# Experts' stage of a two-block model: rows written back half a block later, slot lists four experts at a time, inner columns stored in the order of their transposes

## Chip, cores and metric

The kernel runs on 1 core of one Trainium2 chip. The metric is the device time of one execution in microseconds (us), the median of several; less is better.

## What is computed

Two transformer blocks on 256 tokens of width 1024 in 32-bit floats. The first block's second layer has a mixture of experts, and the change lies there: each token goes to 2 of 8 experts, each expert is a gated network of inner width 3584, and the results are weighted and added to the tokens. Cut to that part:

```python
def moe_swiglu(h, w_router, w_gate, w_up, w_down):
    ...
    logits = (xt @ w_router).astype(jnp.float32)
    top_logit, top_idx = lax.top_k(logits, TOP_K)
    gates = jax.nn.softmax(top_logit, axis=-1)
    ...
    xs = xt_pad[tok_buf].reshape(n_blocks, EXPERT_BLOCK, D)

    def expert_block(args):
        xb, e = args
        return swiglu(xb, w_gate[e], w_up[e], w_down[e])

    ys = lax.map(expert_block, (xs, block_expert)).reshape(rows, D)
    ys = ys * gate_buf[:, None].astype(ys.dtype)
    out = jnp.zeros((T + 1, D), ys.dtype).at[tok_buf].add(ys)[:T]
    return out.reshape(B, S, D)

def swiglu(h, w_gate, w_up, w_down):
    return (jax.nn.silu(h @ w_gate) * (h @ w_up)) @ w_down
```

Before the experts come attention, a dense network and a convolution; after them a second block with two kinds of attention and a dense network.

## The kernel before

**Precision and weights.** Each large product is made of three matmuls (`mm3`, lines 408 to 410): high half times high half, low times high, high times low. All weights come through one stream (`Stream`). SP issues transfers of 1 MB into a ring of raw buffers (tile `wraw`, line 93; 13 buffers in the experts' stage). ScalarE makes the high half of a unit (`whi`, line 107), VectorE subtracts it from the raw weights for the low half (`wlo`, line 122). There are five pairs of `whi` and `wlo`; the stream prepares up to four units ahead of TensorE. In the experts' stage a unit is one slice of 128 rows by 1024 columns, which feeds six matmuls.

**An expert.** Its inner width is cut into blocks 0 to 3 (three of 1024 columns, one of 512). For each block TensorE does, in this order: the gate column into PSUM banks 0 and 1 (`expert_col(gb, ...)`), the up column into banks 2 and 3, then the down product of the block before (`gemm_row` with `prev`), which adds into banks 4 and 5. ScalarE applies the activation to the gate (line 1634), VectorE multiplies it with up (line 1640); both write the tile `grow`. `turn_pairs` then transposes the block's inner values through banks 2 and 3 (line 1621) and splits them into `hth` and `htl` (`split`, lines 389 and 390) for the next block's down product. The down weights are stored in pairs of rows, so the inner columns are turned in even and odd halves: the transposes read `grow` with a stride of two words.

**Handing over.** In block 0 of the next expert the last down product of the one before ends. `rows_of` then copies its rows from banks 4 and 5 into `xn` as high and low halves; `places` makes the slot pattern `ptok` from the slot list; `combine(..., n)` writes one half (n) of the columns back to the tokens: four matmuls of `xn` with `ptok` (line 1537) and two VectorE updates of `h` (line 1540). Half 0 stands at the end of block 0, half 1 behind the gate column of block 1.

**Slot lists.** `slots` finds for each expert which token lies in which slot. It compares (tile `oneb`, line 1490), multiplies with the token numbers (line 1495) and writes `slotv` and `slotr`. `fetch` gathers the next expert's rows by `slotr` on POOL (line 1502), and `turned` transposes them in block 3. All eight experts' lists are made at the end of expert 0's block 1, with the gate weights (`gates`) and the counts (`counts`).

The order on each engine is the order of the code: the schedule is written by hand, and only semaphores delay an instruction.

Of the kernel before, what the change touches and what calls it, by code (L numbers as in the profile page):

```python
# [10 lines left out]
F32 = mybir.dt.float32  # L11
F32R = mybir.dt.float32r
BF = mybir.dt.bfloat16
I32 = mybir.dt.int32
U32 = mybir.dt.uint32
AF = mybir.ActivationFunctionType
OP = mybir.AluOpType
# [4 lines left out]
D = 1024  # L22
# [7 lines left out]
NE = 8  # L30
# [133 lines left out]
def two_blocks(tc, A, out):  # L164
# [14 lines left out]
    def bank(i, shape=(128, 512)):  # L179
        return psp.tile(list(shape), F32, name=f"b{i}", tag=f"b{i}", bufs=1)  # L180
# [126 lines left out]
    R = {}  # L307
# [80 lines left out]
    def split(src, hi_, lo_):  # L388
        S.activation(hi_, src, AF.Copy)  # L389
        V.tensor_tensor(lo_, src, hi_.bitcast(F32), op=OP.subtract)  # L390

    def turn(*a):
        run(turns(*a))
# [48 lines left out]
    def gemm_row(o, ht, chunks, first, last, outer=False, tbs=(0, 1), lead=0):  # L442

        th, tl = ht
        nch = len(chunks)

        def one(u, i, tb, n):
            wh, wl = u
            c = chunks[i]
            mm3(o[tb][n], th[:, c, tb * 128:tb * 128 + 128], tl[:, c, tb * 128:tb * 128 + 128],  # L450
                wh[:, 0, n * 512:n * 512 + 512], wl[:, 0, n * 512:n * 512 + 512],
                first and i == 0, last and i == nch - 1)

        if outer:


            us = []
            for tb in tbs:
                seq = [(n, i) for i in range(nch if tb != tbs[-1] else lead) for n in range(2)]
                seq += [(n, i) for n in range(2) for i in range(len(seq) // 2, nch)]  # L460
                for j, (n, i) in enumerate(seq):
                    if tb == tbs[0] and i >= len(us):
                        us += W.take(1 if lead else nch)
                    one(us[i], i, tb, n)
                    if tb == tbs[-1] and n == 1:
                        W.done(1)
                    if j % 2:
                        yield
        else:
            for i in range(nch):  # L470
                u = W.take(1)[0]
                for tb in tbs:
                    for n in range(2):
                        one(u, i, tb, n)
                    if tb == tbs[-1]:
                        W.done(1)
                    yield

    def run(g):
        for _ in g:  # L480
            pass
# [958 lines left out]
    def gates():  # L1440
        V.tensor_tensor(gg[:, :, 0], mxv[:, :, 1], mxv[:, :, 0], op=OP.subtract)
        S.activation(gg[:, :, 0], gg[:, :, 0], AF.Exp)
        V.tensor_scalar(gg[:, :, 1], gg[:, :, 0], 1.0, None, op0=OP.add)
        V.reciprocal(gg[:, :, 1], gg[:, :, 1])
        V.tensor_tensor(gg[:, :, 2], gg[:, :, 0], gg[:, :, 1], op=OP.mult)
        for tb in range(2):
            V.tensor_scalar(gate[:, tb], oh[:, tb, 0], gg[:, tb, 1:2], None, op0=OP.mult)
            V.scalar_tensor_tensor(gate[:, tb], oh[:, tb, 1], gg[:, tb, 2:3], gate[:, tb], op0=OP.mult, op1=OP.add)
# [31 lines left out]
                  xe[1][:, g * 4:g * 4 + 4])  # L1480
        return xe

    def slots():

        b = bank(7)
        for e0 in range(0, NE, 4):
            ps = []
            for tb in range(2):
                p = mp.tile([128, 4, 128], BF, name="oneb")
                V.tensor_tensor(p, iota[:, None, 1:129].to_broadcast([128, 4, 128]),  # L1490
                                place[:, tb, e0:e0 + 4, None].to_broadcast([128, 4, 128]), op=OP.is_equal)
                ps.append(p)
            for x in range(4):
                for tb in range(2):
                    PE.matmul(b[:, e0 + x:e0 + x + 1], ps[tb][:, x], tokv[:, tb:tb + 1], start=tb == 0, stop=tb == 1)
        V.tensor_copy(slotv, b[:, 0:NE])
        V.tensor_scalar(slotr, slotv, -1.0, 0.0, op0=OP.add, op1=OP.max)

    def fetch(e):

# [4 lines left out]
    def turned(x):  # L1505
        xe = new_xe()
        turn(x, 8, xe[0], xe[1], 0, 0, [6, 7])
        return xe

    def places(e):  # L1510

        pt = mp.tile([128, T], F32R, name="ptok", bufs=1)
        V.tensor_scalar(pt, iota[:, 1:257], slotv[:, e:e + 1], None, op0=OP.is_equal)
        return pt
# [9 lines left out]
    def rows_of(acc):  # L1524

        y = [scr.tile([128, D], F32R, name="xn") for i in range(2)]
        for n in range(2):
            c = slice(n * 512, n * 512 + 512)
            split(acc[n], y[0][:, c], y[1][:, c])
        return y  # L1530

    def combine(e, y, pt, n, tbs=(0, 1)):

        for tb in tbs:
            b = bank(6 + (tb + n) % 2)
            for i, v in enumerate(y):
                PE.matmul(b, pt[:, tb * 128:tb * 128 + 128], v[:, n * 512:n * 512 + 512], start=i == 0,
                          stop=i == len(y) - 1)
            hv = h[:, tb, n * 512:n * 512 + 512]
            V.scalar_tensor_tensor(hv, b, gate[:, tb, e:e + 1], hv, op0=OP.mult, op1=OP.add)  # L1540

    def counts():
        cnt = m1.tile([128, 8], F32, name="cnt")
        b = bank(6)
        for tb in range(2):
            PE.matmul(b[:, 0:8], onesb, sel[:, tb], start=tb == 0, stop=tb == 1)
        mxc = m1.tile([128, 1], F32, name="mxc")
        V.tensor_copy(cnt, b[:, 0:8])
        V.reduce_max(mxc, cnt, axis=AX.X)
        mci = m1.tile([128, 1], I32, name="mci")  # L1550
        V.tensor_copy(mci, mxc)
        return mci
# [54 lines left out]
    def expert_col(bks, xe, n):  # L1607

        if n == 512:
            run(gemm_col([bks[0]], xe, n, tbs=(0,)))  # L1610
        else:
            run(gemm_row([bks], xe, list(range(8)), True, True, tbs=(0,)))

    def turn_pairs(sg, n, ht):


        v = sg[:, 0:n].rearrange("t (q p c) -> t q c p", p=128, c=2)
        for q in range(0, n // 256, 2):
            b = bank(2 + q // 2)
            for x in range(4):  # L1620
                PE.transpose(b[:, x * 128:x * 128 + 128], v[:, q + x // 2, x % 2], ident)
            split(b.rearrange("p (j t) -> p j t", t=128), ht[0][:, 2 * q:2 * q + 4], ht[1][:, 2 * q:2 * q + 4])

    prev = last = None
    nfi = len(exp_blocks)
    for e in range(NE):
        xe = xes.pop(e)
        for fi, (c0, n) in enumerate(exp_blocks):
            hs = [slice(x, x + 512) for x in range(0, n, 512)]
            gb, ub = [bank(0), bank(1)], [bank(2), bank(3)]  # L1630
            expert_col(gb, xe, n)
            sg = growp.tile([128, D], F32, name="grow")
            for x, c in enumerate(hs):
                S.activation(sg[:, c], gb[x], AF.Silu)
            if last is not None:
                combine(*last, 1)
                last = None
            expert_col(ub, xe, n)
            for x, c in enumerate(hs):
                V.tensor_tensor(sg[:, c], ub[x], sg[:, c], op=OP.mult)  # L1640
            if fi == nfi - 1 and e + 1 < NE:
                xes[e + 1] = turned(xg)
            if prev is not None:
                pe_, pacc, pht, pfi, pn = prev
                run(gemm_row([pacc], pht, list(range(pn // 128)), pfi == 0, pfi == nfi - 1, tbs=(0,)))
                if pfi == nfi - 1:
                    last = (pe_, rows_of(pacc), places(pe_))
            if e == 0 and fi == 1:
                gates()
                mci = counts()  # L1650
                slots()
                gcol = const.tile([128, 16], F32, name="gcol")
                for i, nm in enumerate(("mixg", "ffng")):
                    V.scalar_tensor_tensor(gcol[:, 8 * i:8 * i + 8], colsA[:, 8 + 24 * i:16 + 24 * i], 1.0,
                                           P[:, R[nm]:R[nm] + 8], op0=OP.add, op1=OP.mult)
            if fi == min(e, 1) ^ 1 and e + 1 < NE:
                xg = fetch(e + 1)
            if fi == 0:
                acc = [bank(4), bank(5)]
            ht = tuple(mp.tile([128, 8, 128], F32R, name=f"ht{x}", bufs=1) for x in "hl")  # L1660
            turn_pairs(sg, n, ht)
            prev = (e, acc, ht, fi, n)
            if last is not None:
                combine(*last, 0)
    pt = places(NE - 1).bitcast(F32)
    overflow()
    W.hold = True
    for j, _ in enumerate(gemm_row([acc], prev[2], list(range(prev[4] // 128)), False, True, outer=True, tbs=(0,),
# [428 lines left out]
```

## Time and profile before

| | before |
|---|---|
| median of 3 runs | 1856.91 us (1853.91 to 1859.42) |
| profiled execution | 1855.81 us, span 1854.0 us |
| granted TensorE clock, mean | 0.987 |
| TensorE matmuls busy | 1792.2 us, 97% of the span |
| VectorE busy | 1472.1 us, 79% |
| ScalarE busy | 1230.0 us, 66% |
| read from memory | 504.93 MB, 273 GB/s over the span |

The span is the profiled execution from its first to its last instruction; the rest of its time lies around it. Shares of the span are means over stages with different limits: the experts' stage runs from about 515 to 1500 us, and there VectorE and the memory traffic are busier than the table says. A TensorE that is shown as busy has pipelined matmuls whose ends are modelled, so the distance from start to start tells more than the duration.

### The profile page before, as it was taken

What the parts mean: (1) busy time and instruction counts of PE and PEld (TensorE: products, weight loads), DVE (VectorE), ACT (ScalarE), POOL (GpSimd) and SP (SyncE); (2) the same over time, 40 slices, a digit from 0 to 9 for tenths busy, and PEclk for the clock granted to TensorE, in tenths of its full rate; (3) what the DMA queues carried; (4) which work ended last, traced back from release to release, by engine and by line L of the source; (5) the groups of instructions that cost most, each with busy time, mean ns of one, the idle gap of its engine ahead of it and who ended that gap; (6) DMA issues with size and microseconds to landing.
All of it is one profiled execution on the core that took longest, in us unless ns stands there. A gap on an engine that the chain in (4) does not pass through costs nothing. (4 is left out here: it accounts for less than half of the span.)

```text
span 1854.0 us, 23616 instructions
## 1 busy us (share of the span) xinstructions
PE 1792.2 (97%) x8614; PEld 1488.0 (80%) x8614; DVE 1472.1 (79%) x1759; ACT 1230.0 (66%) x1597; POOL 47.4 (3%) x72
## 2 busy tenths in 40 slices
PE   7999999999998999999999999999999989999998
PEld 6788888889787878888788788887887867778886
DVE  5556988688788999999999999999999974477553
ACT  5644444476477778878788778787887866556442
POOL 1100000000100000000000000000000010010000
PEclk9999999999999999999999999999999999999999
DMA  7324998562598999999999999999999735237540
GB/s 276 137 80 158 396 352 296 182 217 80 206 345 315 382 353 360 383 345 367 369 360 379 358 364 377 344 361 363 357 367 357 274 110 172 91 102 264 191 160 23
DMA packets 162740, 508.65 MB, mean 274 GB/s; under 512 B 8452, under 2 KB 26040, under 8 KB 148280
## 3 DMA queue, kind: packets, MB, share of 16 engines
q1 hardware_dynamic: 160200, 499.37, 73.8%
q0 software_dynamic: 2128, 7.18, 1.2%
q8 instruction: 69, 1.13, 0.2%
q10 hardware_dynamic: 288, 0.52, 0.1%
q14 instruction: 55, 0.45, 0.1%
HBM read 504.93 MB, written 2.11 MB: 273 GB/s over the span
## 5 line engine op out<-in xcount | busy, mean ns | idle before, releaser
L122 DVE TENSOR_TENSOR wlo<-wraw,whi 128x1024 fp32r<-128x1024 f32 (+1 forms) x894 | 1063.8, 1220 | 178.7 <-ACT whi L107 132.3
L107 ACT ACTIVATE whi<-wraw 128x1024 fp32r<-128x1024 f32 (+1 forms) x894 | 935.0, 1059 | 304.9 <-PE b L409 280.7
L408 PE MATMUL b<-whi,xeh 128*128 128x512 f32 x896 | 352.2, 393 | 0.0
L410 PE MATMUL b<-wlo,xeh 128*128 128x512 f32 x896 | 350.3, 391 | 0.0
L409 PE MATMUL b<-whi,xel 128*128 128x512 f32 x896 | 350.2, 391 | 0.0
L408 PE MATMUL b<-whi,hth 128*128 128x512 f32 x664 | 262.6, 395 | 0.9 <-ACT hth L389 0.9
L408 PE MATMUL b<-whi,xth 128*128 128x512 f32 (+2 forms) x656 | 257.1, 392 | 6.3 <-ACT xth L389 2.3
L409 PE MATMUL b<-whi,htl 128*128 128x512 f32 x664 | 261.4, 394 | 0.4 <-DVE htl L390 0.4
L410 PE MATMUL b<-wlo,hth 128*128 128x512 f32 x664 | 261.5, 394 | 0.0
L409 PE MATMUL b<-whi,xtl 128*128 128x512 f32 (+2 forms) x656 | 251.6, 384 | 1.7 <-DVE xtl L390 0.9
L410 PE MATMUL b<-wlo,xth 128*128 128x512 f32 (+2 forms) x656 | 251.2, 383 | 1.1 <-DVE wlo L122 1.1
L410 PEld LDWEIGHTS b<-wlo,xeh 128*128 128x128 f32 x896 | 168.7, 188 | 35.2
L408 PEld LDWEIGHTS b<-whi,xeh 128*128 128x128 f32 x896 | 169.2, 189 | 34.6
L409 PEld LDWEIGHTS b<-whi,xel 128*128 128x128 f32 x896 | 168.9, 189 | 34.6
L408 PEld LDWEIGHTS b<-whi,xth 128*128 128x128 f32 x656 | 125.8, 192 | 32.1 <-ACT xth L389 3.8
L408 PEld LDWEIGHTS b<-whi,hth 128*128 128x128 f32 x664 | 126.3, 190 | 27.4 <-ACT hth L389 1.4
L409 PEld LDWEIGHTS b<-whi,htl 128*128 128x128 f32 x664 | 126.1, 190 | 27.0 <-DVE htl L390 1.1
L410 PEld LDWEIGHTS b<-wlo,hth 128*128 128x128 f32 x664 | 126.2, 190 | 26.7
L410 PEld LDWEIGHTS b<-wlo,xth 128*128 128x128 f32 x656 | 125.6, 191 | 25.6 <-DVE wlo L122 2.5
L409 PEld LDWEIGHTS b<-whi,xtl 128*128 128x128 f32 x656 | 125.6, 191 | 24.6 <-DVE xtl L390 2.7
L389 ACT ACTIVATE hth<-b 128x512 fp32r<-128x512 f32 (+1 forms) x84 | 45.9, 591 | 70.8 <-PE b L401 38.6
L390 DVE TENSOR_TENSOR htl<-b,hth 128x512 fp32r<-128x512 f32 (+1 forms) x84 | 54.1, 681 | 39.8 <-ACT hth L389 39.8
(357 smaller groups left out, 1399.9 us busy)
## 6 DMA issues: line engine op xcount, KB each, us to landing
wraw<-in_moe_w_gate_dram SPq DMA_DIRECT2D x112, 1024.0 KB
wraw<-in_moe_w_up_dram SPq DMA_DIRECT2D x112, 1024.0 KB
wraw<-in_moe_w_down_dram SPq DMA_DIRECT2D x112, 1024.0 KB
wraw<-in_w_ff_dram SPq DMA_DIRECT2D x32, 1024.0 KB
adw<-in_ada_w_dram SPq DMA_DIRECT2D x24, 1024.0 KB
wraw<-in_w_in_dram SPq DMA_DIRECT2D x12, 1024.0 KB
wraw<-in_ffn_w_gate_dram SPq DMA_DIRECT2D x11, 1024.0 KB
wraw<-in_ffn_w_up_dram SPq DMA_DIRECT2D x11, 1024.0 KB
```

Source lines behind the costliest of these rows:

```text
L107: nc.scalar.activation(h, r, AF.Copy)
L122: self.nc.vector.tensor_tensor(l, r, h.bitcast(F32), op=OP.subtract)
L389: S.activation(hi_, src, AF.Copy)
L390: V.tensor_tensor(lo_, src, hi_.bitcast(F32), op=OP.subtract)
L408: PE.matmul(o, xh, wh, start=first, stop=False)
L409: PE.matmul(o, xl, wh, start=False, stop=False)
L410: PE.matmul(o, xh, wl, start=False, stop=last)
```

## The change

The half-0 write-back moves from the end of block 0 to behind the gate column of block 1, and half 1 from there to behind the up column. The `ptok` pattern is made in block 2 of the expert itself. The slot lists are made in two goes of four experts (expert 0 and expert 1), the compare in block 0, the matmuls in block 1. The activation and the product write `grow` in the order in which it is turned, so they read PSUM with a stride of two words and the transposes read contiguous columns. The first block's transposes move behind the next gate column, into banks 6 and 7. The gather of the next rows is issued in block 2. The core of the diff:

```diff
-    def slots():
+    def slots(e0):
+        ps = []
+        for tb in range(2):
+            p = mp.tile([128, 4, 128], BF, name="oneb")
+            V.tensor_tensor(p, iota[:, None, 1:129].to_broadcast([128, 4, 128]),
+                            place[:, tb, e0:e0 + 4, None].to_broadcast([128, 4, 128]), op=OP.is_equal)
+            ps.append(p)
+        yield
         b = bank(7)
...
+        for x in range(4):
             for tb in range(2):
+                PE.matmul(b[:, x:x + 1], ps[tb][:, x], tokv[:, tb:tb + 1], start=tb == 0, stop=tb == 1)
+        V.tensor_copy(slotv[:, e0:e0 + 4], b[:, 0:4])
+        V.tensor_scalar(slotr[:, e0:e0 + 4], slotv[:, e0:e0 + 4], -1.0, 0.0, op0=OP.add, op1=OP.max)
+        yield
...
-    def turn_pairs(sg, n, ht):
-        v = sg[:, 0:n].rearrange("t (q p c) -> t q c p", p=128, c=2)
-        for q in range(0, n // 256, 2):
-            b = bank(2 + q // 2)
-            for x in range(4):
-                PE.transpose(b[:, x * 128:x * 128 + 128], v[:, q + x // 2, x % 2], ident)
-            split(b.rearrange("p (j t) -> p j t", t=128), ht[0][:, 2 * q:2 * q + 4], ht[1][:, 2 * q:2 * q + 4])
+    def pairs(x):
+        return x.rearrange("t (q p c) -> t q c p", p=128, c=2)
+    def turn_pairs(sg, n, ht, bk):
+        turn(sg, n // 128, ht[0], ht[1], 0, 0, bk)
...
+        sv4 = [sg[:, x:x + 512].rearrange("t (q c p) -> t q c p", p=128, c=2) for x in hs]
+        for x, v in enumerate(sv4):
+            S.activation(v, pairs(gb[x]), AF.Silu)
+        if later is not None:
+            later()
+            later = None
+        if last is not None:
+            combine(*last, 0)
+        expert_col(ub, xe, n)
+        for x, v in enumerate(sv4):
+            V.tensor_tensor(v, pairs(ub[x]), v, op=OP.mult)
+        if last is not None:
+            combine(*last, 1)
+            last = None
...
-                    last = (pe_, rows_of(pacc), places(pe_))
+                last = (pe_, rows_of(pacc), pt)
...
+        if e < 2 and fi in (0, 1):
+            next(sl[e])
+        if fi == 2:
+            if e + 1 < NE:
+                xg = fetch(e + 1)
+            pt = places(e)
...
-            if last is not None:
-                combine(*last, 0)
```

On VectorE, at the end of block 0 of expert 1 and into block 1, the kernel before has this order (`xn` are the low halves of expert 0's rows, `htl` those of the transposes, `h` the tokens, `wlo` the low halves of weights):

```order
L122 TENSOR_TENSOR wlo<-wraw,whi 128x1024 x4
L390 TENSOR_TENSOR xn<-b_4835,xn 128x512
L390 TENSOR_TENSOR xn<-b_4836,xn 128x512
L1513 TENSOR_SCALAR ptok<-iota,slotv 128x256
L390 TENSOR_TENSOR htl<-b_5932,hth 128x512
L390 TENSOR_TENSOR htl<-b_5939,hth 128x512
L1540 SCALAR_TENSOR_TENSOR h<-b_5946,gate,h 128x512
L1540 SCALAR_TENSOR_TENSOR h<-b_5950,gate,h 128x512
```

And the changed kernel at the same place:

```order
L122 TENSOR_TENSOR wlo<-wraw,whi 128x1024 x4
L390 TENSOR_TENSOR xn<-b_4839,xn 128x512
L390 TENSOR_TENSOR xn<-b_4840,xn 128x512
L1488 TENSOR_TENSOR oneb<-iota,place 128x512 x2
L390 TENSOR_TENSOR htl<-b_5922,hth 128x512
L390 TENSOR_TENSOR htl<-b_5929,hth 128x512
L122 TENSOR_TENSOR wlo<-wraw,whi 128x1024 x8
L1541 SCALAR_TENSOR_TENSOR h<-b_6031,gate,h 128x512
L1541 SCALAR_TENSOR_TENSOR h<-b_6035,gate,h 128x512
L122 TENSOR_TENSOR wlo<-wraw,whi 128x1024 x8
L1647 TENSOR_TENSOR grow<-b_5938,grow 128x512
L1647 TENSOR_TENSOR grow<-b_5939,grow 128x512
```

The pattern `ptok` has left this place, the first two updates of `h` stand eight conversions later, and in expert 1 alone two compare patterns have come in. The other two updates follow the last product shown.

On TensorE, at the same boundary, the kernel before:

```order
L410 MATMUL b_4836<-wlo,hth 128x512
L1621 MATMUL b_5932<-ident,grow 128x128 x4
L1621 MATMUL b_5939<-ident,grow 128x128 x4
L1537 MATMUL b_5946<-xn,ptok 128x512 x2
L1537 MATMUL b_5950<-xn,ptok 128x512 x2
L408 MATMUL b_5954<-whi,xeh 128x512
```

The changed kernel there:

```order
L410 MATMUL b_4840<-wlo,hth 128x512
L401 MATMUL b_5922<-ident,grow 128x128 x4
L401 MATMUL b_5929<-ident,grow 128x128 x4
L408 MATMUL b_5936<-whi,xeh 128x512
L409 MATMUL b_5936<-whi,xel 128x512
```

and a gate column later:

```order
L409 MATMUL b_5937<-whi,xel 128x512
L410 MATMUL b_5937<-wlo,xeh 128x512
L1538 MATMUL b_6031<-xn,ptok 128x512 x2
L1538 MATMUL b_6035<-xn,ptok 128x512 x2
L408 MATMUL b_5938<-whi,xeh 128x512
```

The four row matmuls have moved from between the transposes and the gate column to between the gate and the up column.

On VectorE, at the end of expert 0's block 1, the kernel before makes the patterns and the lists in one go (`cnt` and `mci` belong to the counts):

```order
L1548 COPY cnt<-b_5136 128x8
L1549 TENSOR_REDUCE mxc<-cnt 128x1
L1551 CAST mci<-mxc 128x1
L1490 TENSOR_TENSOR oneb<-iota,place 128x512 x4
L1496 COPY slotv<-b_5144 128x8
L1497 TENSOR_SCALAR slotr<-slotv 128x8
```

The changed kernel has there:

```order
L1549 COPY cnt<-b_5140 128x8
L1550 TENSOR_REDUCE mxc<-cnt 128x1
L1552 CAST mci<-mxc 128x1
L1663 SCALAR_TENSOR_TENSOR gcol<-colsA,P 128x8 x2
L1496 COPY slotv<-b_5151 128x4
L1497 TENSOR_SCALAR slotr<-slotv 128x4
```

The compare patterns stand before this place now: two of them behind the product of block 0, the other two in expert 1, as shown above.

## Rows read from the trace of the kernel before

**Rows 1.** Timeline, POOL: one gather; start, duration, idle time before and releaser.

```profile
1118.81 0.94 POOL L1502 DMA_INDIRECT zN<-zD,slotr  x1 [121.54 <-PE b L401]
```

**Rows 2.** Windows, one expert: length, PE, PEld, DVE, ACT, POOL busy, clock, DMA share, GB/s.

```profile
1000.00:1122.48 122.48, 120.76 (x549) 100.45 (x549) 113.39 (x109) 97.22 (x102) 0.94 (x1) 1.00 0.98 366
```

**Rows 3.** Waits from 600 to 1450: who waited for whom, us, times, longest.

```profile
SPq L93 <- DVE wlo L122: 722.0, 292, 5.8
ACT whi L107 <- PE b L409: 142.1, 424, 2.5
...
PE b L1537 <- ACT whi L107: 12.0, 7, 1.7
```

**Rows 4.** Timeline: two gate transfers are issued, and the gate column that uses them starts.

```profile
666.08 2.64 SPq L93 DMA_DIRECT2D wraw<-in_moe_w_gate_dram  x2
...
705.38 0.48 PE L408 MATMUL b<-whi,xeh 128*128 128x512 f32 x1
```

**Rows 5.** Timeline, PE and DVE: the end of expert 1's block 0.

```profile
667.10 1.11 PE L1621 MATMUL b<-ident,grow 128*128 128x128 f32 x8
...
668.24 1.29 DVE L390 TENSOR_TENSOR xn<-b,xn 128x512 fp32r<-128x512 f32 x2
...
669.43 0.35 DVE L1513 TENSOR_SCALAR ptok<-iota,slotv 128x256 fp32r<-128x256 f32 x1
...
669.93 1.17 PE L1537 MATMUL b<-xn,ptok 128*128 128x512 f32 x4 [1.72 <-ACT whi L107]
...
670.94 0.39 PE L408 MATMUL b<-whi,xeh 128*128 128x512 f32 x1
...
672.32 0.39 PE L408 MATMUL b<-whi,xeh 128*128 128x512 f32 x1
```

**Rows 6.** Timeline, PE: the second half of the same rows, behind the gate column.

```profile
681.84 1.07 PE L1537 MATMUL b<-xn,ptok 128*128 128x512 f32 x4
...
682.75 0.39 PE L408 MATMUL b<-whi,xeh 128*128 128x512 f32 x1
```

**Rows 7.** Timeline, PE: eight transposes at stride two, the next matmul, eight contiguous ones.

```profile
615.66 1.11 PE L1621 MATMUL b<-ident,grow 128*128 128x128 f32 x8
616.53 0.48 PE L408 MATMUL b<-whi,xeh 128*128 128x512 f32 x1
...
627.55 1.03 PE L401 MATMUL b<-ident,zN 128*128 128x128 f32 x8
```

**Rows 8.** Groups from 600 to 1450: count, busy us, mean ns, idle before.

```profile
L122 DVE TENSOR_TENSOR wlo<-wraw,whi 128x1024 fp32r<-128x1024 f32 x585 | 695.5, 1223 | 53.9 <-ACT whi L107 18.7
...
L1640 DVE TENSOR_TENSOR grow<-b,grow 128x512 f32<-128x512 f32 x49 | 31.7, 683 | 0.0
L1621 PEld LDWEIGHTS b<-ident,grow 128*128 128x128 f32 x196 | 27.8, 205 | 2.2
...
L1540 DVE SCALAR_TENSOR_TENSOR h<-b,gate,h 128x512 f32<-128x512 f32 x28 | 19.7, 745 | 0.0
...
L401 PEld LDWEIGHTS b<-ident,zN 128*128 128x128 f32 x56 | 6.5, 140 | 0.9
```

**Rows 9.** Timeline, PE: counts, slot lists and the next gate column, expert 0.

```profile
572.91 0.20 PE L1546 MATMUL b<-sel,onesb 128*128 128x8 bf16 x2
...
576.67 0.18 PE L1495 MATMUL b<-tokv,oneb 128*128 128x1 bf16 x1 [3.56 <-DVE oneb L1490]
...
577.27 0.33 PE L1495 MATMUL b<-tokv,oneb 128*128 128x1 bf16 x7 [0.42 <-DVE oneb L1490]
...
580.78 0.77 PE L408 MATMUL b<-whi,xeh 128*128 128x512 f32 x1
```

**Rows 10.** Windows behind that place, columns as in rows 2.

```profile
580.00:582.00 2.00, 2.00 (x9) 1.80 (x8) 0.90 (x2) 1.43 (x3) 1.14 (x2) 0.50 0.19 73
...
584.00:586.00 2.00, 2.00 (x8) 1.56 (x7) 1.22 (x1) 0.71 (x2) 0.00 (x0) 0.69 0.74 266
```

**Rows 11.** Timeline, PE: expert 0's first transposes.

```profile
539.02 1.34 PE L1621 MATMUL b<-ident,grow 128*128 128x128 f32 x8 [1.43 <-DVE grow L1640]
```

More of the change, by code (lines that the diff above doesn't have):

```diff
@@ L1481, in gather @@
         return xe
-    def slots():
+    def slots(e0):
[6 more added lines that the diff above has]
+        yield
         b = bank(7)
-        for e0 in range(0, NE, 4):
-            ps = []
+        for x in range(4):
             for tb in range(2):
[L1489 to L1492, printed above, removed]
-            for x in range(4):
[L1494 to L1497, printed above, removed]
+                PE.matmul(b[:, x:x + 1], ps[tb][:, x], tokv[:, tb:tb + 1], start=tb == 0, stop=tb == 1)
+        V.tensor_copy(slotv[:, e0:e0 + 4], b[:, 0:4])
+        V.tensor_scalar(slotr[:, e0:e0 + 4], slotv[:, e0:e0 + 4], -1.0, 0.0, op0=OP.add, op1=OP.max)
+        yield
     def fetch(e):
@@ L1612, in expert_col @@
             run(gemm_row([bks], xe, list(range(8)), True, True, tbs=(0,)))
-    def turn_pairs(sg, n, ht):
-        v = sg[:, 0:n].rearrange("t (q p c) -> t q c p", p=128, c=2)
-        for q in range(0, n // 256, 2):
-            b = bank(2 + q // 2)
-            for x in range(4):
-                PE.transpose(b[:, x * 128:x * 128 + 128], v[:, q + x // 2, x % 2], ident)
-            split(b.rearrange("p (j t) -> p j t", t=128), ht[0][:, 2 * q:2 * q + 4], ht[1][:, 2 * q:2 * q + 4])
+    def pairs(x):
+        return x.rearrange("t (q p c) -> t q c p", p=128, c=2)
@@ L1624, in two_blocks @@
+    def turn_pairs(sg, n, ht, bk):
+        turn(sg, n // 128, ht[0], ht[1], 0, 0, bk)
     prev = last = None
     nfi = len(exp_blocks)
[L1626 to L1634, printed above, removed]
-            if last is not None:
[L1636 to L1646, printed above, removed]
-                    last = (pe_, rows_of(pacc), places(pe_))
[L1648 to L1656, printed above, removed]
-                xg = fetch(e + 1)
[L1658 to L1663, printed above, removed]
-                combine(*last, 0)
@@ L1665, in two_blocks, with later @@
-    pt = places(NE - 1).bitcast(F32)
+    steps = [(e, fi) for e in range(NE) for fi in range(nfi)]
+    later = None
+    sl = [slots(0), slots(4)]
+    for e, fi in steps:
+        c0, n = exp_blocks[fi]
+        if fi == 0:
+            xe = xes.pop(e)
+        hs = range(0, n, 512)
+        gb, ub = [bank(0), bank(1)], [bank(2), bank(3)]
+        expert_col(gb, xe, n)
+        sg = growp.tile([128, D], F32, name="grow")
+        sv4 = [sg[:, x:x + 512].rearrange("t (q c p) -> t q c p", p=128, c=2) for x in hs]
[3 more added lines that the diff above has]
+            later()
+            later = None
+        if last is not None:
[6 more added lines that the diff above has]
+            last = None
+        if fi == nfi - 1 and e + 1 < NE:
+            xes[e + 1] = turned(xg)
+        if prev is not None:
+            pe_, pacc, pht, pfi, pn = prev
+            run(gemm_row([pacc], pht, list(range(pn // 128)), pfi == 0, pfi == nfi - 1, tbs=(0,)))
+            if pfi == nfi - 1:
+                last = (pe_, rows_of(pacc), pt)
+        if e == 0 and fi == 1:
+            gates()
+            mci = counts()
+            gcol = const.tile([128, 16], F32, name="gcol")
+            for i, nm in enumerate(("mixg", "ffng")):
+                V.scalar_tensor_tensor(gcol[:, 8 * i:8 * i + 8], colsA[:, 8 + 24 * i:16 + 24 * i], 1.0,
+                                       P[:, R[nm]:R[nm] + 8], op0=OP.add, op1=OP.mult)
+        if e < 2 and fi in (0, 1):
+            next(sl[e])
+        if fi == 2:
+            if e + 1 < NE:
+                xg = fetch(e + 1)
+            pt = places(e)
+        if fi == 0:
+            acc = [bank(4), bank(5)]
+        ht = tuple(mp.tile([128, 8, 128], F32R, name=f"ht{x}", bufs=1) for x in "hl")
+        if prev is None:
+            def later(a=(sg, n, ht, [6, 7])):
+                turn_pairs(*a)
+        else:
+            turn_pairs(sg, n, ht, [2, 3])
+        prev = (e, acc, ht, fi, n)
@@ L1666, in two_blocks @@
+    pt = pt.bitcast(F32)
     overflow()
```

## Prediction

> **What bounds the kernel now.** I read the windows first, cut to one expert: gathers of successive experts start 0.94 + 121.54 = 122.48 us apart [rows 1], and in such a stretch TensorE is busy 120.76 us, VectorE 113.39 and ScalarE 97.22, while the DMA engines show 0.98 at 366 GB/s [rows 2]. Three things look full, so the waits decide which one sets the pace. Over seven experts ScalarE's conversion of the weights waits for TensorE to hand slots back (424 times), the DMA queue waits for VectorE to free raw buffers, and no row has an engine waiting for weights from memory. TensorE itself waits at one line alone, the matmul that writes rows back (L1537): 7 times, 12.0 us [rows 3]. TensorE bounds the experts' stage; what counts is what stands between its big matmuls.
>
> The transfers are early too. The two gate tiles issued at 666.08 are those of block 2 of that expert: 13 raw buffers hold its block 1 (gate 4, up 4, down 4) and one more. TensorE begins on them at 705.38 [rows 4], 39 us later.
>
> The timeline shows what stands between the big matmuls. At an expert's first block boundary the transposes begin at 667.10 and the next gate matmul at 670.94; between them the row matmuls wait until 669.93. The profile names a ScalarE instruction as releaser, but it was long done: VectorE's low half of the rows (from 668.24) and the slot pattern ptok (669.43, 0.35 us) end just before [rows 5]. VectorE is behind there, after four conversions. Later in the same block four row matmuls whose inputs are old take 682.75 - 681.84 = 0.91 us and wait for nothing [rows 6].
>
> **The change part by part.**
>
> *Rows go back later.* Both halves now stand where the second half stood: behind a column of matmuls, with rows and ptok long ready. The boundary shrinks from 3.84 us to its eight transposes, 616.53 - 615.66 = 0.87 [rows 7], and the four matmuls cost 0.91 elsewhere [rows 6]. Gain 3.84 - 0.87 - 0.91 = 2.06 us; seven experts hand over this way (the eighth's tail code is unchanged): **14.4 us**. The ptok it waited for is now made a block or more earlier. The second half's updates now stand behind the up products on VectorE, ahead of the next weights' low halves; that cover must be priced. From the end of the up column, VectorE finishes the conversion it is in (1.14 us later, taken from the boundary, where its next work starts at 668.24 after the column's end at 667.10), then two products (0.68 each), two updates (0.75 each) and one conversion (1.22) [rows 8]: 5.2 us. TensorE needs that fifth low half after four row matmuls (0.91) and four units of 672.32 - 670.94 = 1.38 each, and two matmuls more (0.46): 6.9 us [rows 5, 6]. Cover is left: 1.7 us, or 0.85 per product.
>
> *Slot lists by fours.* In expert 0's block 1 TensorE goes from 572.91 to 580.78, 7.87 us, with counts, slots and transposes; it waits 3.56 us for the first compare pattern alone, and VectorE is then in a row of small operations [rows 9]. The patterns are now written a block earlier, so TensorE finds ten short matmuls with inputs ready (0.20 us for the two of the counts, and about 0.4 for eight where seven took 0.33) and the transposes, 0.8: gain 7.87 - 1.4 = 6.5. Four experts' matmuls move to expert 1's block 1: minus 0.4. The clock comes on top. After that stall the granted clock is 0.50 from 580 on and 0.69 over 584 to 586, so the half level lasts to 584 + 0.62 x 2 = 585.2 [rows 10]. [...] Sum: **8.3 us**. The two compare patterns on VectorE (expert 0 and expert 1, block 0) lie beside a gate column of 8 x 1.38 = 11 us.
>
> *The first block's transposes* wait 1.43 us for the product and then take 1.34 by their row [rows 11]. Moved behind the next gate column, and contiguous, they wait for nothing and their row should read 1.03, as below: 1.43 + 1.34 - 1.03 = **1.7 us**. Their halves are wanted an up column (11 us) later.
>
> *Inner columns in turned order.* The product is now contiguous for the transposes: eight of them took 1.11 us strided and 1.03 contiguous [rows 7], and their weight loads 205 and 140 ns [rows 8]. So 0.08 per eight; an expert has 28 transposes, eight experts 224 or 28 groups, less the two counted above: 26 x 0.08 = **2.1 us**. In exchange ScalarE's activation and VectorE's product read PSUM two words apart. No row has such a read. Bounds: nothing (0.68 us a product), or at the far end one word in the time of two, 1.37. Nearest is the weight load with the same stride, 205/140 = 1.46 times, or 1.0 us. All three stay within the 0.85 of cover above, so in the sum it is zero; without cover 0.32 x 49 products = 16 us would show.
>
> [...]
>
> *Moved without price.* The gather of the next rows is issued later in program order, but it starts when its buffer is free and POOL has waited 121.54 us for that [rows 1]; the rows are wanted most of an expert later. Transposes at later blocks also wait for their bank's up column, 50 matmuls back.
>
> **Sum.** 14.4 + 8.3 + 1.7 + 2.1 = 26.5 us. The profiled execution took 1855.8 (span 1854.0 and 1.8 around it), giving 1829.3; the median of the runs, 1856.9, lies 1.1 higher, giving 1830.4. I say 1830. Runs differ by 0.3%, some 5.6 us, and that is also what I call no change.
>
> **Rivals.**
> - *Products stall a little.* If the strided read costs over 0.85 us more per product, or the burst meets a conversion that is later than I reckon, TensorE waits at the end of an up column or at the boundary instead. For: VectorE is at 93% and was the one that held the boundary. Against: at the old boundary VectorE had rows, ptok, two subtractions of the transposes and two updates in one burst; the new one has four of these six, and once, in expert 1, the two compare patterns. At 0.3 us per block over 28 blocks the gain falls by 8: 1838. Half of the gain would be 1843.
> - *VectorE becomes the bound, and the time rises.* TensorE's need per expert falls to 122.48 - 2.06 - 0.28 = 120.1 us; VectorE's is 113.39. From 6.7/7 = 0.96 us more per product (1.64, or 2.4 times) VectorE sets the pace; from (122.48 + 1.25 - 113.39)/7 = 1.48 more (2.16, or 3.2 times), where 1.25 is the startup's 10.0 spread over eight experts, all the gain is gone. At 4 times, 2.73 us, it would be 56 products x 0.57 = 32 us slower than before, 1889. [...] Against: the one strided read of the trace, the weight load, cost 1.46 times [rows 8].
> - *Memory becomes the bound.* The stage would need 366 x 122.48 / 120.1 = 373 GB/s, with the DMA engines at 0.98 already [rows 2]. If 366 were the ceiling, the stage would lose 2.3 us per expert against the buffers' 39 us [rows 4]: they would last through all eight (19 us), and nothing is lost. Only if the buffers refill too late at the start does some come back: the startup's 10 us, 1840. For: the share. Against: no wait for memory in any row.
> [...]
>
> **How the numbers follow.** The forecast has 0.80 (its own range 1826 to 1834), a little stall 0.10, memory 0.04, VectorE as the bound 0.04 (0.03 of it slower than before), and 0.02 for a gain larger than reckoned. The range reaches to 1842 for the first two rivals and to 1823 for the runs' spread and the last: 1823 to 1842 leaves out under 2 in 10. Faster by over 0.3% means under 1851.3: 0.94; within 0.3%, which only part of the last two cases reaches: 0.03; slower: 0.03.
>
> **What the profile after would show.** The row matmuls (L1538) with no idle time before them; gathers 120.1 us apart; no stretch at 0.50 near 575 and no pause over 2 us there; contiguous transposes at 140 ns a load; VectorE's product (L1647) between 0.68 and 1.0 us and ScalarE's activation between 0.59 and 0.86. I am wrong if the product is over 1.6 us, if matmuls with wlo begin to wait for VectorE, or if conversions wait for weights to land.

## The result, and the profile after

The changed kernel takes 1830.24 us (median of 4 runs, 1827.98 to 1831.55) against 1857.11 for the kernel before on the same chip (4 runs); the ratio is 0.9855, 95% interval 0.9837 to 0.9873. The forecast was 1830, its range 1823 to 1842. The profiled execution took 1831.55, its span is 1829.8.

The experts' stage alone, from its first gate matmul to its last transposes, took 1495.83 - 515.58 = 980.25 us before and takes 1470.43 - 517.17 = 953.26 now: 27.0 us less, where the sum said 26.5. Outside the stage the two profiled executions differ the other way: the stage begins 1.6 us later after the change, and what follows it takes 1.2 us longer, so the spans differ by 24.2 us. These are the two ends before, in the timeline of TensorE:

```profile
515.58 0.48 PE L408 MATMUL b<-whi,xeh 128*128 128x512 f32 x1
...
1495.83 0.63 PE L1621 MATMUL b<-ident,grow 128*128 128x128 f32 x4
```

And after:

```profile
517.17 0.48 PE L408 MATMUL b<-whi,xeh 128*128 128x512 f32 x1
...
1470.43 0.60 PE L401 MATMUL b<-ident,grow 128*128 128x128 f32 x4
```

One expert in the windows (columns as in [rows 2]) and the gather that tells the period (as [rows 1]):

```profile
1000.00:1120.15 120.15, 120.15 (x549) 99.80 (x549) 112.70 (x108) 96.97 (x103) 0.94 (x1) 1.00 0.99 372
```

```profile
1100.42 0.94 POOL L1503 DMA_INDIRECT zN<-zD,slotr  x1 [119.21 <-PE b L401]
```

The period is 0.94 + 119.21 = 120.15 us instead of 122.48, and TensorE is shown busy in all of it. The answer to [rows 3], the waits from 600 to 1430, has no line of the row matmuls (L1538) any more and still none of weights from memory:

```profile
ACT whi L107 <- PE b L409: 127.7, 405, 1.2
ACT hth L389 <- PE b L401: 20.5, 21, 1.2
DVE wlo L122 <- ACT whi L107: 19.7, 33, 0.8
```

The boundary of [rows 5] and the two write-backs in the timeline:

```profile
657.69 1.03 PE L401 MATMUL b<-ident,grow 128*128 128x128 f32 x8
658.49 0.48 PE L408 MATMUL b<-whi,xeh 128*128 128x512 f32 x1
...
669.50 1.07 PE L1538 MATMUL b<-xn,ptok 128*128 128x512 f32 x4
...
670.40 0.39 PE L408 MATMUL b<-whi,xeh 128*128 128x512 f32 x1
...
681.28 1.07 PE L1538 MATMUL b<-xn,ptok 128*128 128x512 f32 x4
682.14 1.28 DVE L1647 TENSOR_TENSOR grow<-b,grow 128x512 f32<-128x512 f32 x2
682.19 0.39 PE L408 MATMUL b<-whi,hth 128*128 128x512 f32 x1
...
683.34 1.40 DVE L1541 SCALAR_TENSOR_TENSOR h<-b,gate,h 128x512 f32<-128x512 f32 x2
```

From the first transpose to the gate matmul it is 658.49 - 657.69 = 0.80 us, where [rows 5] had 3.84; each set of four row matmuls takes 0.90 or 0.91, as [rows 6]. VectorE's burst behind the up column (two products, two updates) stands there as reckoned, and TensorE goes on beside it.

The answer to [rows 9], counts, slot lists and transposes of expert 0, and the windows over the place of [rows 10]:

```profile
572.59 0.20 PE L1547 MATMUL b<-sel,onesb 128*128 128x8 bf16 x2
...
572.66 0.34 PE L1495 MATMUL b<-tokv,oneb 128*128 128x1 bf16 x8
...
572.86 1.07 PE L401 MATMUL b<-ident,grow 128*128 128x128 f32 x8
...
573.68 0.48 PE L408 MATMUL b<-whi,xeh 128*128 128x512 f32 x1
```

```profile
570.00:580.00 10.00, 10.00 (x59) 8.25 (x58) 9.21 (x23) 9.05 (x11) 2.03 (x2) 1.00 1.01 357
```

The stretch is 573.68 - 572.59 = 1.09 us instead of 7.87, and the granted clock stays at 1.00. The first block's transposes (as [rows 11]) wait for nothing. Before, with the big matmuls on either side:

```profile
537.21 0.39 PE L410 MATMUL b<-wlo,xeh 128*128 128x512 f32 x1
...
540.12 0.49 PE L408 MATMUL b<-whi,xeh 128*128 128x512 f32 x1
```

And after:

```profile
549.68 0.39 PE L410 MATMUL b<-wlo,xeh 128*128 128x512 f32 x1
549.91 1.03 PE L401 MATMUL b<-ident,grow 128*128 128x128 f32 x8
550.70 0.48 PE L408 MATMUL b<-whi,xeh 128*128 128x512 f32 x1
```

And the groups from 600 to 1430 that answer to [rows 8]:

```profile
L1647 DVE TENSOR_TENSOR grow<-b,grow 128x512 f32<-128x512 f32 x47 | 30.4, 683 | 0.0
L1639 ACT ACTIVATE grow<-b 128x512 f32<-128x512 f32 x49 | 28.9, 589 | 4.5 <-PE b L410 3.7
...
L401 PEld LDWEIGHTS b<-ident,grow 128*128 128x128 f32 x196 | 23.0, 140 | 3.5
```

The activation before, in its groups from 600 to 1430:

```profile
L1634 ACT ACTIVATE grow<-b 128x512 f32<-128x512 f32 x47 | 27.7, 590 | 4.5 <-PE b L410 3.7
```

The product that reads PSUM two words apart takes 683 ns, what the contiguous one took, and the activation 589 where it took 590; the transposes' weight loads fell from 205 to 140.

### The profile page after: what moved, and what is told of

It is laid out like the page before. It is cut to its first block, busy times and chain, and to the rows that moved or that the text cites. A ratio compares the mean times of both kernels' runs of the same rounds, so it can differ in the third digit from the quotient of the medians.

```text
span 1829.8 us, 23609 instructions
## 1 busy us (share of the span) xinstructions
PE 1784.6 (98%) x8614; PEld 1480.0 (81%) x8614; DVE 1465.2 (80%) x1761; ACT 1228.2 (67%) x1597; POOL 47.4 (3%) x72
## 5 line engine op out<-in xcount | busy, mean ns | idle before, releaser
L410 PEld LDWEIGHTS b<-wlo,hth 128*128 128x128 f32 x664 | 125.9, 190 | 26.5
```

Of the source, the lines that this page charges most:

```text
L410: PE.matmul(o, xh, wl, start=False, stop=last)
```

## The experiments

**Theory:** TensorE sets the pace of the stage, and what was taken from between its big matmuls is the gain, part by part. **Rivals:** VectorE or memory holds the stage, so a wait only moves; the clock falls whatever the pause; the strided read costs time that the cover hides.

A gain worked out from a ratio lies up to 2 us from the difference of the medians beside it, and its interval is some 3 to 6 us wide. The length of the experts' stage in each profile, given behind the last experiment, is a second measure.

**The rows alone, later.** The kernel before with this edit:

```diff
             expert_col(gb, xe, n)
...
-            if last is not None:
-                combine(*last, 1)
-                last = None
+            if last is not None:
+                combine(*last, 0)
             expert_col(ub, xe, n)
             for x, c in enumerate(hs):
                 V.tensor_tensor(sg[:, c], ub[x], sg[:, c], op=OP.mult)
+            if last is not None:
+                combine(*last, 1)
+                last = None
...
-                    last = (pe_, rows_of(pacc), places(pe_))
+                    last = (pe_, rows_of(pacc), pt)
...
+            if fi == 2:
+                pt = places(e)
...
-            if last is not None:
-                combine(*last, 0)
...
```

> The kernel before with one part of the change: rows go back behind the gate column (first half) and behind the up column (second half), and ptok is made in block 2. Theory (TensorE sets the pace, and each hand-over held it 2.06 us): the seven boundaries shrink from 3.84 to 0.87 us, the row matmuls show no idle time, gathers follow each other 120.4 us apart, and the median falls by 14.4 us to about 1842.5. Rival (VectorE's or the transfers' pace holds the stage, so the wait only moves): boundaries shrink, but matmuls elsewhere begin to wait for wlo or for weights, and the time falls by under 5 us.

Measured: 1842.11 us (5 runs) against 1857.85 (15 runs), ratio 0.9926 (0.9912 to 0.9941), so 13.7 us less (11.0 to 16.3). The gathers are 120.55 us apart:

```profile
1105.09 0.94 POOL L1502 DMA_INDIRECT zN<-zD,slotr  x1 [119.61 <-PE b L401]
```

The theory holds: the wait is gone and nothing else began to wait. The period is 0.15 us above the 120.4 expected; why stays open. The pause for the slot lists is still there, and the windows behind it show how much of the low clock TensorE meets:

```profile
574.00:576.00 2.00, 1.58 (x14) 1.50 (x15) 0.98 (x5) 0.10 (x1) 0.00 (x0) 0.50 0.61 235
576.00:578.00 2.00, 2.00 (x9) 1.72 (x8) 1.31 (x2) 1.74 (x3) 1.56 (x2) 0.61 0.13 20
```

The clock is at half until 576 + 0.78 x 2 = 577.56 here, and the gate column starts at 576.37: TensorE loses 0.6 us by it (half of the 1.19), not 2.2 as in [rows 10]. The restarts in the kernels with the columns alone and the pattern alone lie like this one: by the same windows the half level ends there at 583.6 and 578.96, and the gate columns start at 582.43 and 577.75. The half level is 6.8 us long before (from 578.4 to 585.2) and here (from 570.7 to 577.6); only its place beside the restart differs.

**The slot lists alone, by fours.** The kernel before with the new `slots` and this:

```diff
                 mci = counts()
-                slots()
...
+            if e < 2 and fi in (0, 1):
+                next(sl[e])
             if fi == min(e, 1) ^ 1 and e + 1 < NE:
                 xg = fetch(e + 1)
```

> The kernel before with the slot lists made by four experts, compare patterns a block earlier, and nothing else. Theory: the stretch in expert 0's block 1 shrinks from 7.87 to about 1.5 us and the granted clock no longer falls to 0.50 behind it; the median falls by 8.3 us to about 1849. Rival (the clock falls anyway, the pause is not its cause): 6.1 us, 1851, with a stretch at 0.50 near 575 to 585.

Measured: 1850.94 us (5 runs), ratio 0.9956 (0.9941 to 0.9971), 8.2 us less (5.4 to 11.0). No fall of the clock:

```profile
574.00:584.00 10.00, 10.00 (x49) 8.38 (x49) 9.48 (x24) 8.80 (x11) 2.04 (x2) 1.00 1.02 387
```

The time alone does not decide, since the rival's 6.1 lies within the interval; the clock does. It falls to 0.50 in this pause before [rows 10] and with the rows alone, its half level ends behind it with the columns and the pattern alone as given above, and it stays at 1.00 at this place here and in the changed kernel, so the rival falls. The row matmuls wait 12.0 us in 7 times there, as before: the slot lists take nothing from the rows' part.

**The columns alone, in turned order.** The kernel before with this edit (`quads` is the view of `grow` by q, c, p; `pairs` is that of the diff under The change):

```diff
...
+        turn(sg, n // 128, ht[0], ht[1], 0, 0, [2, 3])
...
-                S.activation(sg[:, c], gb[x], AF.Silu)
+                S.activation(quads(sg[:, c]), pairs(gb[x]), AF.Silu)
...
-                V.tensor_tensor(sg[:, c], ub[x], sg[:, c], op=OP.mult)
+                V.tensor_tensor(quads(sg[:, c]), pairs(ub[x]), quads(sg[:, c]), op=OP.mult)
```

> The kernel before with the inner columns written in the order of their transposes, and nothing else. Theory: the product stays between 0.68 and 1.0 us behind its cover, weight loads of transposes fall from 205 to 140 ns, eight transposes from 0.87 to 0.79 us; 2.2 us in all, about 1855, which the timing can't tell from no change but the distances in the trace can. [...]

Measured: 1854.48 us (11 runs), ratio 0.9984 (0.9975 to 0.9993), 3.0 us less (1.3 to 4.6). The groups from 600 to 1450:

```profile
L1639 DVE TENSOR_TENSOR grow<-b,grow 128x512 f32<-128x512 f32 x49 | 31.7, 682 | 0.0
...
L401 PEld LDWEIGHTS b<-ident,grow 128*128 128x128 f32 x196 | 23.0, 140 | 3.6
```

The rival of a strided read that costs time behind its cover falls: the product takes 682 ns, where it took 683.

**The slot pattern alone, early.** The last two edits of the rows' diff (`pt` from block 2), with both write-backs at their old places.

> The kernel before with ptok made in block 2 and everything else at its old place. Theory (the row matmuls waited for the last of VectorE's work in order, rows and then ptok): the first row matmul starts at once, the second waits for the low half of the rows alone, and a boundary falls from 3.84 to about 2.7 us; 8 us in all, 1849. Rival (ScalarE's work held it, as the profile names it): nothing changes, 1857.

Measured: 1847.44 us (5 runs, spread 1844.21 to 1853.03), ratio 0.9954 (0.9939 to 0.9969), 8.5 us less (5.8 to 11.3). The boundary in the timeline:

```profile
662.53 1.11 PE L1621 MATMUL b<-ident,grow 128*128 128x128 f32 x8
...
663.40 0.48 PE L1537 MATMUL b<-xn,ptok 128*128 128x512 f32 x1
663.67 1.28 DVE L390 TENSOR_TENSOR xn<-b,xn 128x512 fp32r<-128x512 f32 x2
...
664.17 1.07 ACT L107 ACTIVATE whi<-wraw 128x1024 fp32r<-128x1024 f32 x1
664.40 0.98 PE L1537 MATMUL b<-xn,ptok 128*128 128x512 f32 x3 [0.53 <-DVE xn L390]
...
665.22 0.40 PE L408 MATMUL b<-whi,xeh 128*128 128x512 f32 x1
```

665.22 - 662.53 = 2.69 us: 1.15 less than 3.84, seven times. The first row matmul starts before VectorE has begun on the rows' low halves, and the second when the first of them is there. ScalarE's conversion, which the profile of before names as releaser, begins after the first row matmul here and ends after the last has begun: it held nothing. ptok stood last in VectorE's order, and by its place this 0.35 us instruction cost more than half of the 2.06.

**The product made twice, and three times.** Two kernels from the changed one, which make each product once or twice more into scratch (the extra results are used nowhere; the second kernel has `range(2)`):

```diff
...
+            for _ in range(1):
+                V.tensor_tensor(work.tile([128, 512], F32, name="sq").rearrange("t (q c p) -> t q c p", p=128, c=2),
+                                pairs(ub[x]), v, op=OP.mult)
             V.tensor_tensor(v, pairs(ub[x]), v, op=OP.mult)
```

> The changed kernel with each product made twice (once more into scratch), as if the strided read took about double: some 0.65 us more for each of 56 products on VectorE. Theory (1.7 us of cover per pair at the worst place, 120.1 us needed by TensorE against about 118 by VectorE): no matmul waits, the time stays within 3 us of 1830. Rival (VectorE already sets the pace at 93%): 56 x 0.65 = 36 us more, 1866, or a part of it.

> The changed kernel with each product made three times, some 1.3 us more for each. Theory (VectorE becomes the bound from 0.96 us more): VectorE needs about 122.5 us per expert, TensorE waits for wlo, and the time rises by about 2.4 x 8 = 19 us to 1849. Rival (cover is larger than reckoned): it stays under 1835.

Measured: twice 1831.32 us (4 runs), ratio to the kernel before 0.9871 (0.9856 to 0.9886), where the changed kernel had 0.9855; three times 1849.02 (6 runs), ratio 0.9968 (0.9956 to 0.998), of 1855.32 for the kernel before on that chip. With the product twice, one expert in the windows and the largest line of TensorE's waits from 600 to 1400:

```profile
1000.00:1120.15 120.15, 120.15 (x550) 99.86 (x549) 115.59 (x115) 96.97 (x103) 0.94 (x1) 1.00 0.98 372
```

```profile
PEld b L410 <- DVE wlo L122: 0.9, 1, 0.9
```

Three times, the same two views, and the period:

```profile
1000.00:1122.24 122.24, 120.98 (x550) 99.62 (x549) 119.24 (x122) 96.96 (x103) 1.02 (x1) 1.00 0.95 366
```

```profile
PE b L410 <- DVE wlo L122: 9.2, 13, 1.7
DVE wlo L122 <- ACT whi L107: 9.0, 13, 0.8
```

```profile
1105.68 1.02 POOL L1503 DMA_INDIRECT zN<-zD,slotr  x1 [121.22 <-PE b L401]
```

The places of these waits in one expert, in the timeline of TensorE:

```profile
1029.07 0.50 PE L410 MATMUL b<-wlo,xeh 128*128 128x512 f32 x1 [0.48 <-DVE wlo L122]
...
1053.71 0.50 PE L410 MATMUL b<-wlo,hth 128*128 128x512 f32 x1 [0.78 <-DVE wlo L122]
```

0.65 us more per product is hidden, 1.3 us more is not: the period rises from 120.15 to 122.24, and matmuls with `wlo` wait for VectorE. The cover of 0.85 us that the prediction gave lies between. Both kernels bear out its size: at the second place, behind the up column of block 1 with the burst that it priced, some 2.6 us of extra products per pair left 0.78 us of wait, so the cover was about 1.8 us per pair (an estimate) where 1.7 was reckoned. The first place lies in the gate column of block 1, 7.5 us behind the boundary; for it the prediction had no sum.

The rival that VectorE sets the pace is false for the changed kernel. The kernel with three products met the 19 us expected of it, but not by VectorE being full: VectorE itself still waits for ScalarE 13 times, 9.0 us in all, about twice in each expert, so it catches up in between. What ran out there is the cover of single bursts. From which length VectorE would set the pace of a whole expert no run shows. The busy time shown for VectorE grew by less than the work added (2.9 us per expert with the product twice, where seven times 0.65 are 4.6), so the busy time shown does not tell here how full VectorE is.

**Nine raw buffers in place of thirteen.** The changed kernel with

```diff
-NX, NB, NY, NC = 3, 5, 0, 1
+NX, NB, NY, NC = 3, 1, 0, 1
```

> The changed kernel with 9 raw buffers for the weights in place of 13 (4 MB less ahead). Theory (transfers have time to spare and TensorE sets the pace): no conversion waits for weights, within 3 us of 1830. Rival (memory is at its ceiling and the stage lives on its buffers): conversions wait for weights to land in the experts' stage and the time rises by 5 us or more.

Measured: 1829.86 us (4 runs), ratio 0.9858 (0.9843 to 0.9873), as the changed kernel. One expert:

```profile
1000.00:1120.15 120.15, 120.15 (x550) 99.83 (x549) 112.69 (x108) 96.92 (x103) 0.94 (x1) 1.00 0.99 373
```

The period is the same with 4 MB less ahead, and no conversion waits for weights there. But the time of this kernel could hardly have shown a ceiling: nine buffers hold about 26 us of work (an estimate: 120.15 us for an expert's 42 transfers of 1 MB, so 2.86 each), and a ceiling at 366 GB/s would have used up 19 us in the whole stage. What tells is the rate over the stage, in the windows before and after:

```profile
600.00:1430.00 830.00, 817.99 (x3713) 680.16 (x3712) 769.44 (x729) 658.38 (x692) 4.68 (x5) 1.00 0.97 363
```

```profile
600.00:1430.00 830.00, 830.00 (x3796) 689.32 (x3795) 779.20 (x744) 669.91 (x706) 4.68 (x5) 1.00 0.99 371
```

The faster kernel draws 371 GB/s over 830 us where the slower drew 363, and nine buffers draw 371 as well. So a share of 0.97 or 0.98 was not the ceiling; whether 0.99 is, no run shows.

**The stage in each profile.** From the first gate matmul to the last transposes, read as the two ends above, in us:

| kernel | first | last | stage | against before |
|---|---|---|---|---|
| before | 515.58 | 1495.83 | 980.25 | |
| changed | 517.17 | 1470.43 | 953.26 | -26.99 |
| rows alone | 511.12 | 1476.30 | 965.18 | -15.07 |
| slot lists alone | 516.13 | 1488.01 | 971.88 | -8.37 |
| columns alone | 517.28 | 1495.23 | 977.95 | -2.30 |
| pattern alone | 512.51 | 1483.19 | 970.68 | -9.57 |
| product twice | 514.51 | 1468.90 | 954.39 | -25.86 |
| product three times | 509.55 | 1481.98 | 972.43 | -7.82 |
| nine buffers | 517.21 | 1470.51 | 953.30 | -26.95 |

Each is one profile. The rows, the columns and the pattern alone hold 1.6 us that is not theirs, since their half level behind the pause cost 0.6 and not 2.2. Without it the rows give 13.4 and the pattern 7.9; the columns lost as much again at another boundary (last section) and stay at 2.3.

## Why the prediction was right, point by point

- **What bounds.** TensorE did: the period fell by 2.33 us, and 2.06 + 0.28 = 2.34 were reckoned. The rival of memory is refuted by the rate, which rose with TensorE's need, the one of VectorE by the product made twice.
- **Rows, 14.4 us.** The seven boundaries gave 3.84 - 0.80 - 0.91 = 2.13 each, of which 0.08 belongs to the columns: 14.4. Alone they measured 13.7 (11.0 to 16.3). That VectorE's order held them was right. One sentence was wrong: ScalarE's conversion was not "long done" at that boundary; it ended at 669.82, 0.11 us ahead of the row matmuls' start, which may be why the profile names it. The early ptok shows that it held nothing. Its line, in ScalarE's timeline of the kernel before:

```profile
668.75 1.07 ACT L107 ACTIVATE whi<-wraw 128x1024 fp32r<-128x1024 f32 x1
```

- **Slot lists, 8.3 us.** 7.87 - 1.09 = 6.78 of pause, less 0.25 for the eight matmuls in expert 1 (0.4 was taken), plus 2.2 of clock: 8.7. Alone 8.2 (5.4 to 11.0), and 8.4 in the stage. That the pause brought the clock down was right: it was at 0.50 behind it before and with the rows alone, and at 1.00 in the changed kernel and with the slot lists alone. The 2.2 are half of the stretch from 580.78 to 585.2. That just half of it comes back no run shows: before, ten matmuls from 580.78 take 4.42 us at granted clock 0.50 and ten from 616.53 take 2.39 at 1.00, which gives 2.0. The size of the clock's term holds for the one profile that it was read from: the half level lay so beside the restart that it cost 2.2, and in the three other profiles with the pause it cost 0.6, halves of their stretches too. With 0.6 this part would be 7.1 and the whole sum 24.9; the times can't tell the two apart.
- **First transposes, 1.7 us.** From the big matmul before to the one behind, less one matmul's pitch, it was 2.69 and is 0.79: 1.9. Where the other 0.2 comes from is not shown; of this part alone no kernel was run.
- **Columns, 2.1 us.** The distances fell by 0.08 per eight, and alone it measured 3.0 (1.3 to 4.6), in the stage 2.3. Of the three bounds for the strided read the lowest was the true one. The prediction had its nearest row, the strided weight load at 1.46 times, from another engine's path, and it did not carry over. For reads of PSUM at two words by VectorE (683 ns before and after) and ScalarE (590 and 589) these runs show no cost.
- **The sum.** 14.4 + 8.7 + 1.9 + 2.1 = 27.1 against 27.0 in the stage. The parts tried alone give 13.4 + 8.4 + 2.3 there, and with the fourth's 1.9 that is 26.0; where the last 1.0 lies is not shown. The medians moved by 26.9 and the profiled executions by 24.3, so that the median of 1830.24 fell on the forecast of 1830 is in part luck: the parts are good to 1 or 2 us, and the start of the stage shifts by more.
- **Little stall, 0.10.** It did not come: no matmul waits for `wlo` between 600 and 1430. The thrice-made product, with its 0.78 us of wait behind the up column, shows that such a burst can hold TensorE, and that the cover was about as large as reckoned.

## What to carry to other kernels

Where one engine is full, read what stands between its instructions, and for each wait the order of the queue that it waits for: here a 0.35 us pattern at the end of VectorE's order cost about 1.15 us at each boundary, and it could be made at any time before. Put work that needs a result behind a stretch that needs nothing from it, and price the burst that this makes on the other engine against the units that lie ready. Engines that show 93% or 98% busy, as VectorE and the DMA engines here, may still have room: doubling a small instruction on the one tells in one run, and for transfers the rate tells, if it rises when the other engines need more. Before you take buffers away as a test, work out whether the ones left would hide the answer.

## What the runs showed that was not expected

- Reading PSUM two words apart cost VectorE and ScalarE nothing (683 ns before and after; 590 and 589), while the same stride in a weight load cost TensorE 205 against 140 ns.
- Once the clock fell behind a pause of about two microseconds. In the profile of the columns-only kernel the granted clock was 0.57 from 1037 to 1041, behind one of the seven old boundaries, whose row matmuls waited until 1036.35; the profile of before, with the same seven pauses, has 1.00 from 600 to 1430. The columns-only kernel there:

```profile
1034.00:1037.00 3.00, 1.20 (x8) 0.90 (x7) 3.00 (x6) 2.22 (x4) 0.00 (x0) 1.00 1.03 359
1037.00:1041.00 4.00, 4.00 (x13) 3.10 (x12) 3.24 (x5) 1.06 (x1) 0.00 (x0) 0.57 0.92 322
```

  That period was 1.64 us longer than its neighbours (123.81 against 122.17). Why this boundary and not the others stays open.
- The stage's first gate matmul stood between 509.6 and 517.3 us in nine profiles whose code ahead of it does the same work; by the clock's records the half level lasted about 14 us in all before the earliest (product three times, granted clock 0.99 from 0 to 500) and about 31 before the changed kernel's 517.17 (0.97 from 0 to 510). That spread is about as large as the slot lists' whole term, so the terms were read from distances within the stage and not from the total.
